# Strassen sums of the second feed-forward matrix made by adding DMAs instead of VectorE subtractions, with the signs turned and another order of products

## The chip, the cores and the metric

One Trainium2 chip, one of its NeuronCores. The metric is the device time of one execution in microseconds (us), median of several runs; lower is better. The engines are named as in the profile: PE (TensorE matmul, PEld its weight loads), ACT (ScalarE), DVE (VectorE), POOL (GpSimd), SP (SyncE, which issues most DMAs).

## The reference, cut to what matters

```python
x = x + mix @ w_out                                  # attention mix, before this
h2 = rmsnorm(x, norm2_w)
x = x + jnp.square(jax.nn.relu(h2 @ w_ff1)) @ w_ff2  # the feed-forward pair
return rmsnorm(x, final_norm_w)
```

x is 512 x 1024 in fp32, w_ff1 1024 x 4096, w_ff2 4096 x 1024. All products are to fp32 accuracy.

## The kernel before, in words

A product to fp32 accuracy is made of three fast ones. Each weight tile of 128 x 1024 is loaded as fp32 (wraw or w2raw) and cut in two (`parts`): ACT copies it, rounded, into wh, and DVE writes wl = raw - wh. The activations are cut alike (Ah and Al, yh and yl). PE then adds up wh by Ah, wh by Al and wl by Ah in PSUM. One such pair (wh, wl) is called a piece here.

The feed-forward part goes in four chunks (NC = 4, here 0 to 3). A chunk has eight tiles of the first matrix (`ff1`, tiles f of 0 to 31; PE writes bank f, ACT makes relu and square into h), and then one multiplication of a 512 x 1024 activation block by a 1024 x 1024 block of w_ff2 (`ff2`). Since that block is cut in 2 x 2 quadrants on each side, seven products do the work of eight (Strassen, in Winograd's form). The products are numbered 0 to 6. Each takes sums or differences of the activation quadrants (`a_parts`: s1 to s4, from h) and of the weight quadrants (`sums2`: b11, b12, b21, b22, each of two tiles ip = 0, 1). Piece "6.1" below is tile ip = 1 of the weights of product 6. Each product is 24 matmuls, 12 for each half q of its 256 rows. Its PSUM banks are called X, Y, Z and W; when a bank is whole enough, DVE adds it into x3 (`add`), the tile of the result. PE goes one tile of ff1 into the next chunk before each chunk's products, and in the last chunk straight from f = 31 to the products.

The order of all instructions on all engines is set by `Plan`, a small model of the engines that runs while the kernel is built: streams of work (loads, cuts, sums, products) each offer their next instruction, and the one that could start earliest by the model's costs is written next. The order is then fixed; on the chip every engine takes its instructions in that order and waits on semaphores. A stream also takes and gives counted buffers: `big` (23 tiles of 128 x 1024, for raw tiles, pieces and sums), `w` (5 pieces at a time, 10 in the last chunk), `raw2` (loaded w_ff2 tiles, 8) and the PSUM banks.

What the change touches. `fetch2` loads the four quadrants of a chunk with eight SP DMAs. `sums2` waits for them, and DVE makes the four sums as b12 - b11, b22 - that (a tile of its own, t2), t2 - b11 and b21 - t2, two tiles each: 8 subtractions of 128 x 1024 in a chunk. `products` gives the order in which `cut2` cuts the weights and `ff2` multiplies: 0, 1, 2, 3, 4, 5, 6 in chunks 0 to 2, and 0, 4, 1, 6, 2, 3, 5 in chunk 3. In chunk 3 the last additions into x3 feed the final norm: ACT squares and sums a tile (junk), DVE makes the mean (m), ACT and DVE the inverse root (y, tmp), and DVE and ACT the output (of, xw), which SP stores. POOL multiplies four finished halves of x3 by the norm weights (xw, `weighted`), and is otherwise idle in the feed-forward part.

Of the kernel before, what the change touches and what calls it, by code (L numbers as in the profile page):

```python
# [32 lines left out]
class Op:  # L33


    def __init__(self, eng, method, args, kw):
        self.eng, self.method, self.args, self.kw = eng, method, args, kw
        self.out = args[0]
        outs = [args[0]]
        inner = [a for a in list(args[1:]) + [v for k, v in kw.items() if k != "accum_out"] if isinstance(a, bass.AP)]  # L40
        if kw.get("accum_out") is not None:
            outs.append(kw["accum_out"])
        if method == "tensor_tensor_reduce":
            outs.append(inner.pop())
        self.outs = [o.tensor.name for o in outs]
        self.ins = [a.tensor.name for a in inner]
# [24 lines left out]
        if method == "dma_start":  # L71
            self.cost = 0.06
            self.size = 4 * n * args[0].shape[0]


# [114 lines left out]
def hybrid_block_kernel(ctx: ExitStack, tc: tile.TileContext, xT_d, x_d, w0_d, wv_d, wqk_d, wo_d, w1_d, w2_d,  # L190
# [9 lines left out]
    plan = Plan(nc, dict(BANKS, raw=3, w=WPAIRS, big=BIGS, raw2=8, part=5, lev=4, cnt=1))  # L200
    spawn, fire, give = plan.spawn, plan.fire, plan.give
    late = dict(copy=LC, tt=LT)

# [104 lines left out]

    quads = {}

    def fetch2():
        yield ("wait", ("raw", ("1", 5)))
        for c in range(NC):
            for q in ((0, 0), (1, 0), (1, 1), (0, 1)):
                for ip in range(2):
                    yield ("take", "raw2")
                    yield ("take", "big")
                    t = quads[c, q, ip] = big("w2raw")
                    yield SP.dma_start(t, w2_d[c, q[0], q[1], ip])
                fire(("quad", c, q))  # L320
            spawn(sums2(c), 4)

    def sums2(c):

        for q in ((0, 0), (1, 0), (1, 1), (0, 1)):
            yield ("wait", ("quad", c, q))
        b11, b12, b21, b22 = ([quads.pop((c, q, ip)) for ip in range(2)] for q in ((0, 0), (0, 1), (1, 0), (1, 1)))
        t2 = [None, None]
        B[c] = {0: b11, 1: b21, 5: b22, 3: b12, 2: t2, 4: b11, 6: b21}
        for n in (0, 1, 5):  # L330
            fire(("B", c, n))
        if c == NC - 1:
            yield ("prio", 2)
        for ip in range(2):
            yield DVE.tensor_tensor(b12[ip], b12[ip], b11[ip], op=OP.subtract)
            yield ("take", "big")
            t2[ip] = big("t2")
            yield DVE.tensor_tensor(t2[ip], b22[ip], b12[ip], op=OP.subtract)
        fire(("B", c, 2))
        fire(("B", c, 3))  # L340
        yield ("wait", ("cut2", c, 0))
        for ip in range(2):
            yield DVE.tensor_tensor(b11[ip], t2[ip], b11[ip], op=OP.subtract)
        fire(("B", c, 4))
        yield ("wait", ("cut2", c, 1))
        for ip in range(2):
            yield DVE.tensor_tensor(b21[ip], b21[ip], t2[ip], op=OP.subtract)
        fire(("B", c, 6))
        yield ("wait", ("cut2", c, 2))
        give("big")  # L350
        give("big")

    B = {}

    def products(c):


        if c < NC - 1:
            return ((0, "X", True, ((0, 0),)), (1, "Y", True, ((0, 0),)), (2, "X", False, ((0, 1),)), (3, "Z", True, ((1, 1),)),
                    (4, "X", False, ((1, 1),)), (5, "Z", False, ((0, 1),)), (6, "X", False, ((1, 0),)))  # L360
        return ((0, "X", True, ((0, 0),)), (4, "W", True, ((1, 1),)), (1, "Y", True, ((0, 0),)), (6, "W", False, ((1, 0),)),
                (2, "X", False, ((0, 1), (1, 1), (1, 0))), (3, "Z", True, ((1, 1),)), (5, "Z", False, ((0, 1),)))

    def cut2(c):
        for o, (n, *_) in enumerate(products(c)):
# [7 lines left out]
                yield from parts(("2", c, n, ip), B[c][n][ip])  # L373
            fire(("cut2", c, n))
            for _ in range(2):
                if n > 2:
                    give("big")
                    give("raw2")

# [612 lines left out]
    def a_parts(c, h):  # L992
# [28 lines left out]
        for f in range(4):
            yield ("wait", ("h", c, f))
        for ip in range(2):
            yield from split(0, ip, quad(0, one, ip))
        for ip in range(2):
# [3 lines left out]
        yield from urgent(1)  # L1029
        if c == NC - 1:  # L1030
            for ip in range(2):
                yield from split(4, ip, s3[ip])
        yield from urgent(2)
        for f in range(4, 8):
            yield ("wait", ("h", c, f))
        for ip in range(2):
            yield from split(1, ip, quad(1, one, ip))
        if c == NC - 1:
            yield from urgent(3)
            for ip in range(2):  # L1040
                yield from split(6, ip, quad(1, two, ip))
        yield from urgent(4)
        for ip in range(2):
            s1[ip], s2[ip] = new("s1"), new("s2")
            for i in range(2):
                yield DVE.tensor_tensor(s1[ip][:, i], quad(0, two, ip)[i], quad(1, two, ip)[i], op=OP.add)
                yield DVE.tensor_tensor(s2[ip][:, i], s1[ip][:, i], quad(0, one, ip)[i], op=OP.subtract)
        for ip in range(2):
            yield from split(2, ip, s2[ip])
        yield from urgent(5)  # L1050
        for ip in range(2):
            yield from split(3, ip, s1[ip])
        yield from urgent(6)
        for ip in range(2):
            s4[ip] = new("s4")
            for i in range(2):
                yield DVE.tensor_tensor(s4[ip][:, i], quad(1, one, ip)[i], s2[ip][:, i], op=OP.subtract)
        if c < NC - 1:
            for ip in range(2):
                yield from split(4, ip, s3[ip])  # L1060
        for ip in range(2):
            yield from split(5, ip, s4[ip])
        if c < NC - 1:
            for ip in range(2):
                yield from split(6, ip, quad(1, two, ip))

    A = {}
    TAGS = dict(X="s", Y="pt", Z="pt", W="mm")

    def add(c, i, q, acc):  # L1070
        n, b_, _, targets = products(c)[i]
        for blk, half in targets:
            t = 2 * blk + q
            if c == NC - 1 and n != 5:
                yield ("prio", 1.3 + i + 2 * (n == 4))
            yield DVE.tensor_tensor(x3[t, half], acc, x3[t, half], op=OP.add)
# [39 lines left out]
    def ffn():  # L1116
# [219 lines left out]
```

## Time and profile before

| | |
|---|---|
| runs | 595.39, 594.39, 595.22 us, median 595.22 us |
| profiled execution: its span, first to last instruction | 592.2 us |
| median less span: what lies around the span | 3.0 us |
| PE clock granted, mean | 0.996 |
| bytes moved by DMA | 61.91 MB |

The profiled execution's own time is known as its span; the 3.0 us are what the median of the runs has beyond it. In the rows below, a row of a timeline or of the chain of waits starts with its start in the span and its duration, both in us; in a table of windows each engine has its busy time and its count of instructions, and at the end stand the granted clock, the busy share of the DMA engines and their GB/s. A row of the costliest groups or of one tile says how many instructions there are of a form and how long they take.

### The profile page before, as it was taken

The numbers are of one execution on the slowest core, as the hardware profiler recorded it, in microseconds if no ns is written. First come the engines' busy times: TensorE is split into PE (matmuls) and PEld (weight loads), VectorE is DVE, ScalarE is ACT, GpSimd is POOL, SyncE is SP. The second block draws the span as 40 slices with busy tenths as digits, with TensorE's granted clock in tenths as the row PEclk, the third lists the DMA queues.
The fourth block names the chain that finished last, engine by engine and source line by source line (L and its number), as shares of the span: only waits on it lengthen the run. The fifth ranks groups of instructions, "written<-read, shape, count | busy, mean of one in ns | idle before, by whom it ended". The sixth has DMA issues, their size and how long they took to land.

```text
span 592.2 us, 8140 instructions
## 1 busy us (share of the span) xinstructions
PE 579.9 (98%) x3021; PEld 477.9 (81%) x3021; DVE 424.9 (72%) x829; ACT 324.7 (55%) x603; POOL 17.6 (3%) x33
## 2 busy tenths in 40 slices
PE   9999999999999999999999999999999999999993
PEld 8978888778877777899888888888888888888882
DVE  5879995854897824566579954499925799665995
ACT  6744256865687734555456424565244564365534
POOL 6020000000000000000000000000000000000020
PEclk9999999999999999999999999999999999999998
DMA  8921404132314610093104732015521046200003
GB/s 294 346 75 37 141 21 143 53 107 71 109 57 125 246 35 2 11 384 139 37 0 143 243 113 71 1 71 199 191 72 35 2 143 212 72 0 37 1 0 143
DMA packets 20391, 61.91 MB, mean 105 GB/s; under 512 B 2544, under 2 KB 2586, under 8 KB 20352
## 3 DMA queue, kind: packets, MB, share of 16 engines
q1 hardware_dynamic: 19728, 60.37, 29.7%
q0 software_dynamic: 480, 1.02, 0.5%
q8 instruction: 24, 0.39, 0.3%
q14 instruction: 15, 0.12, 0.1%
q10 hardware_dynamic: 144, 0.01, 0.0%
HBM read 59.25 MB, written 2.13 MB: 104 GB/s over the span
## 4 chain that ended last, share of the span: by engine, by line
PE 86%; DVE 10%; ACT 2%; issue 1%
PE f L123 30%; PE f2X L123 11%; PE qkps L123 8%; PE ops L123 7%; PE vps L123 7%; PE f2Z L123 6%; PE f2Y L123 3%; PE po L123 2%; PE ptp L123 2%; PE sps L123 2%; PE av L123 2%; DVE wl L123 2%; DVE x L123 2%; PE lp L123 1%; DVE P L123 1%; DVE Al L123 1%
## 5 line engine op out<-in xcount | busy, mean ns | idle before, releaser
L123 PE MATMUL f<-yh,wh 128*128 128x512 f32 (+1 forms) x288 | 105.3, 366 | 0.0
L123 PE MATMUL f<-yl,wh 128*128 128x512 f32 (+1 forms) x288 | 105.3, 365 | 0.0
L123 PE MATMUL f<-yh,wl 128*128 128x512 f32 (+1 forms) x288 | 105.2, 365 | 0.0
L123 DVE TENSOR_TENSOR wl<-wraw,wh 128x1024 fp32r<-128x1024 f32 (+1 forms) x68 | 78.4, 1161 | 33.5 <-ACT wh L123 28.0
L123 ACT ACTIVATE wh<-wraw 128x1024 fp32r<-128x1024 f32 (+1 forms) x67 | 67.2, 1013 | 60.1 <-PE f L123 24.0
L123 DVE TENSOR_TENSOR wl<-w2raw,wh 128x1024 fp32r<-128x1024 f32 x48 | 59.4, 1243 | 48.2 <-ACT wh L123 44.4
L123 ACT ACTIVATE wh<-w2raw 128x1024 fp32r<-128x1024 f32 x48 | 50.3, 1054 | 48.2 <-PE f L123 38.8
L123 PEld LDWEIGHTS f<-yh,wh 128*128 128x128 f32 x288 | 54.3, 189 | 8.8
L123 PEld LDWEIGHTS f<-yh,wl 128*128 128x128 f32 x288 | 54.3, 189 | 8.7
L123 PEld LDWEIGHTS f<-yl,wh 128*128 128x128 f32 x288 | 54.3, 189 | 8.7
L123 PE MATMUL f2X<-wh,Ah 128*128 128x512 f32 x112 | 43.6, 389 | 0.0
L123 PE MATMUL f2X<-wh,Al 128*128 128x512 f32 x112 | 43.6, 389 | 0.0
L123 PE MATMUL f2X<-wl,Ah 128*128 128x512 f32 x112 | 43.6, 389 | 0.0
L123 PE MATMUL qkps<-xh,wh 128*128 128x512 f32 x96 | 39.8, 415 | 0.0
L123 PE MATMUL qkps<-xh,wl 128*128 128x512 f32 x96 | 37.6, 391 | 0.0
L123 PE MATMUL qkps<-xl,wh 128*128 128x512 f32 x96 | 37.5, 391 | 0.0
L123 ACT ACTIVATE P<-P,mn 128x512 f32<-128x512 f32 (+3 forms) x48 | 26.6, 555 | 9.9 <-DVE mn L123 9.6
L123 DVE CUSTOM_DVE_ANT_0 P<-sps,nb 128x512 f32<-128x512 f32 (+3 forms) x48 | 22.2, 482 | 10.9 <-PE sps L123 10.8
L123 ACT ACTIVATE Ah<-s 128x512 fp32r<-128x512 f32 x32 | 19.6, 621 | 18.5 <-DVE s L123 18.5
L123 ACT ACTIVATE h<-f 128x512 f32<-128x512 f32 x32 | 18.6, 582 | 18.3 <-PE f L123 18.3
L123 PE MATMUL vps<-wh,xh 128*128 128x512 f32 x64 | 27.2, 424 | 0.0
L123 PE MATMUL ops<-wh,mh 128*128 128x512 f32 x64 | 26.1, 407 | 0.0
(223 smaller groups left out, 1191.6 us busy)
## 6 DMA issues: line engine op xcount, KB each, us to landing
wraw<-in_w SPq DMA_DIRECT2D x32, 512.0 KB, 3.3
w2raw<-in_w SPq DMA_DIRECT2D x32, 512.0 KB, 4.0
wraw<-in_wqk SPq DMA_DIRECT2D x12, 512.0 KB, 4.1
wraw<-in_wv SPq DMA_DIRECT2D x8, 512.0 KB, 5.4
wraw<-in_wo SPq DMA_DIRECT2D x8, 512.0 KB, 3.5
nb<-tab SPq DMA_DIRECT2D x12, 256.0 KB, 3.5
wraw<-in_w SPq DMA_DIRECT2D x8, 264.0 KB, 7.0
xT<-in_xT SPq DMA_DIRECT2D x8, 256.0 KB, 7.0
```

Of the source, the lines that this page charges most:

```text
L123: getattr(getattr(self.nc, op.eng), op.method)(*op.args, **op.kw)
```

## The change: what it does

- The weight sums are made by DMAs that POOL issues with `accum_op=add`: such a DMA reads a quadrant from DRAM and adds it to what stands in the tile in SBUF. Quadrant b12 is loaded twice (tiles of products 3 and 4), so a chunk has 10 loads instead of 8, and 8 adding DMAs of 512 KB in chunks 0 to 2 and 12 in chunk 3. The 32 subtractions on DVE, and the tile t2, are gone. `raw2` grows to 10.
- The sums become plain sums: 3 is b12 + b11, 4 is b12 + b22, 2 is b12 + b11 + b22, 6 is 2's sum + b21. In chunks 0 to 2 one tile holds 3, then 2, then 6: each DMA adds in place after the earlier product's piece has been cut from the tile. In chunk 3, 6 is made in the tile of 4 by two more additions (b11, b21), and 3 in the tile of b11.
- The signs move to the activations (s1 is a difference, s4 a sum) and to `add`, which subtracts the bank from x3 for some products.
- Chunks 0 to 2 take the products in the order 0, 3, 2, 1, 4, 5, 6; chunk 3 keeps its order. `a_parts` makes what each product needs in that order. Bank Y moves from the tag pt to o and g.
- `Plan` counts an adding DMA as 1.0 us of POOL, and as a reader of its tile.

```diff
+        self.ins = [a.tensor.name for a in inner] + (self.outs if "accum_op" in kw else [])
...
+            self.cost = 1.0 if "accum_op" in kw else 0.06
...
+    plan = Plan(nc, dict(BANKS, raw=3, w=WPAIRS, big=BIGS, raw2=10, part=5, lev=4, cnt=1))
...
     def sums2(c):
-        for ip in range(2):
-            yield DVE.tensor_tensor(b12[ip], b12[ip], b11[ip], op=OP.subtract)
-            yield ("take", "big")
-            t2[ip] = big("t2")
-            yield DVE.tensor_tensor(t2[ip], b22[ip], b12[ip], op=OP.subtract)
...
+        def plus(n, q):
+            for ip in range(2):
+                yield POOL.dma_start(B[c][n][ip], w2_d[c, q[0], q[1], ip], accum_op=OP.add)
+
+        b = B[c]
+        if c < NC - 1:
+            yield from plus(3, (0, 0))
+            yield from plus(4, (1, 1))
+            yield ("wait", ("cut2", c, 3))
+            b[2] = b[3]
+            yield from plus(2, (1, 1))
+            yield ("wait", ("cut2", c, 2))
+            b[6] = b[2]
+            yield from plus(6, (1, 0))
+        else:
+            yield from plus(4, (1, 1))
+            b[2] = b[3]
+            yield from plus(2, (0, 0))
+            yield ("wait", ("cut2", c, 4))
+            b[6] = b[4]
+            yield from plus(6, (0, 0))
+            yield from plus(2, (1, 1))
+            yield from plus(6, (1, 0))
+            yield ("wait", ("cut2", c, 0))
+            b[3] = b[0]
+            yield from plus(3, (0, 1))
...
-                if n > 2:
+                if n in ((0, 1, 4, 5, 6) if c < NC - 1 else (1, 2, 3, 5, 6)):
                     give("big")
                     give("raw2")
...
+            yield DVE.tensor_tensor(x3[t, half], x3[t, half], acc, op=OP.subtract if half and b_ in "XW" else OP.add)
```

Three places in the built order. First POOL in the last chunk, after the change. Tiles 4870 and 4879 (ip = 0 and 1) hold 4 and then 6, tiles 4819 and 4829 hold 2, tiles 4536 and 4545 hold b11 and then 3. Before the change POOL has nothing at this place, only the four xw multiplications behind it.

```order
L123 DMA w2raw_4870<-in_w2 128x1024
L123 DMA w2raw_4879<-in_w2 128x1024
L123 DMA w2raw_4819<-in_w2 128x1024
L123 DMA w2raw_4829<-in_w2 128x1024
L123 DMA w2raw_4870<-in_w2 128x1024
L123 DMA w2raw_4879<-in_w2 128x1024
L123 DMA w2raw_4819<-in_w2 128x1024
L123 DMA w2raw_4829<-in_w2 128x1024
L123 DMA w2raw_4870<-in_w2 128x1024
L123 DMA w2raw_4879<-in_w2 128x1024
L123 DMA w2raw_4536<-in_w2 128x1024
L123 DMA w2raw_4545<-in_w2 128x1024
```

So between the first addition for 6 (fifth and sixth row) and the second (ninth and tenth) stand the two that finish 2.

Second, ACT and DVE in the last chunk around the cut of 6. Before the change, on ACT: wh_5240 and wh_5259 are pieces 6.0 and 6.1, wh_5275 is 2.0, the h are ff1's results of f = 28 to 31, the Ah cuts for products 1 and 6.

```order
L123 ACTIVATE wh_5240<-w2raw_4807 128x1024
L123 ACTIVATE h_5242<-f1_5199 128x512
L123 ACTIVATE h_5242<-h_5242 128x512
L123 ACTIVATE Ah_5256<-h_5121 128x256
L123 ACTIVATE Ah_5256<-h_5169 128x256
L123 ACTIVATE wh_5259<-w2raw_4822 128x1024
L123 ACTIVATE Ah_5268<-h_5205 128x256
L123 ACTIVATE wh_5275<-t2_4936 128x1024
```

The same place on ACT after the change; 6.0 is wh_5255 and 6.1 wh_5279, from the tiles that POOL's DMAs add to.

```order
L123 ACTIVATE h_5248<-f1_5204 128x512
L123 ACTIVATE h_5248<-h_5248 128x512
L123 ACTIVATE Ah_5265<-h_5134 128x256
L123 ACTIVATE wh_5255<-w2raw_4870 128x1024
L123 ACTIVATE Ah_5265<-h_5175 128x256
L123 ACTIVATE wh_5279<-w2raw_4879 128x1024
L123 ACTIVATE Ah_5286<-h_5208 128x256
L123 ACTIVATE Ah_5286<-h_5248 128x256
```

6.0 has moved behind the last h, and both copies of 6 still stand ahead of the activations' cuts Ah_5286 for product 1.

On DVE before the change the low halves of 6.0 and 6.1 (wl_5241 and wl_5260) both stand ahead of the additions of product 0 (f2X) into x3:

```order
L123 TENSOR_TENSOR wl_5241<-w2raw_4807,wh_5240 128x1024
L123 TENSOR_TENSOR Al_5257<-h_5121,Ah_5256 128x256
L123 TENSOR_TENSOR Al_5257<-h_5169,Ah_5256 128x256
L123 TENSOR_TENSOR wl_5260<-w2raw_4822,wh_5259 128x1024
L123 TENSOR_TENSOR x3_2310<-f2X_5235,x3_2310 128x512
L123 TENSOR_TENSOR Al_5269<-h_5205,Ah_5268 128x256
```

After the change (wl_5256 and wl_5280):

```order
L123 TENSOR_TENSOR wl_5256<-w2raw_4870,wh_5255 128x1024
L123 TENSOR_TENSOR Al_5266<-h_5175,Ah_5265 128x256
L123 TENSOR_TENSOR x3_2310<-x3_2310,f2X_5241 128x512
L123 TENSOR_TENSOR Al_5287<-h_5208,Ah_5286 128x256
L123 TENSOR_TENSOR x3_2314<-x3_2314,f2X_5242 128x512
L123 TENSOR_TENSOR Al_5287<-h_5248,Ah_5286 128x256
L123 TENSOR_TENSOR Al_5306<-h_5134,Ah_5305 128x256
L123 TENSOR_TENSOR Al_5306<-h_5175,Ah_5305 128x256
L123 TENSOR_TENSOR Al_5315<-h_5208,Ah_5314 128x256
L123 TENSOR_TENSOR Al_5315<-h_5248,Ah_5314 128x256
L123 TENSOR_TENSOR wl_5280<-w2raw_4879,wh_5279 128x1024
```

The low half of 6.1 has moved behind the additions of product 0 and six cuts of activations.

Third, DVE where product 3 (f2Z) ends and product 5 waits for its bank. Before:

```order
L123 TENSOR_SCALAR m_5503<-ssq_5495 128x1
L123 TENSOR_TENSOR x3_2325<-f2X_5236,x3_2325 128x512
L123 TENSOR_SCALAR m_5518<-ssq_5514 128x1
L123 TENSOR_TENSOR x3_2322<-f2Z_5483,x3_2322 128x512
L123 TENSOR_TENSOR x3_2327<-f2Z_5484,x3_2327 128x512
```

After:

```order
L123 TENSOR_SCALAR m_5518<-ssq_5510 128x1
L123 TENSOR_TENSOR x3_2325<-x3_2325,f2X_5242 128x512
L123 TENSOR_TENSOR x3_2322<-x3_2322,f2Z_5491 128x512
L123 TENSOR_SCALAR m_5536<-ssq_5532 128x1
L123 TENSOR_TENSOR x3_2327<-x3_2327,f2Z_5492 128x512
```

The first addition of f2Z and the small m, which waits for ACT, have changed places.

More of the change, by code (lines that the diff above doesn't have):

```diff
@@ L45, in __init__ @@
         self.outs = [o.tensor.name for o in outs]
-        self.ins = [a.tensor.name for a in inner]
+        self.ins = [a.tensor.name for a in inner] + (self.outs if "accum_op" in kw else [])
         n = 1
@@ L71, in __init__ @@
         if method == "dma_start":
-            self.cost = 0.06
+            self.cost = 1.0 if "accum_op" in kw else 0.06
             self.size = 4 * n * args[0].shape[0]
@@ L199, in hybrid_block_kernel @@
     BANKS = dict(mm=2, s=2, pt=2, o=1, g=1)
-    plan = Plan(nc, dict(BANKS, raw=3, w=WPAIRS, big=BIGS, raw2=8, part=5, lev=4, cnt=1))
+    plan = Plan(nc, dict(BANKS, raw=3, w=WPAIRS, big=BIGS, raw2=10, part=5, lev=4, cnt=1))
     spawn, fire, give = plan.spawn, plan.fire, plan.give
@@ L309, in hybrid_block_kernel @@
     quads = {}
+    SUMS = {3: (0, 1), 4: (1, 1)}
     def fetch2():
@@ L313, in fetch2 @@
         for c in range(NC):
-            for q in ((0, 0), (1, 0), (1, 1), (0, 1)):
+            B[c] = {}
+            for n, q in ((0, (0, 0)), (1, (1, 0)), (3, (0, 1)), (4, (0, 1)), (5, (1, 1))):
+                t = []
                 for ip in range(2):
@@ L317, in fetch2 @@
                     yield ("take", "big")
-                    t = quads[c, q, ip] = big("w2raw")
-                    yield SP.dma_start(t, w2_d[c, q[0], q[1], ip])
-                fire(("quad", c, q))
+                    t.append(big("w2raw"))
+                    yield SP.dma_start(t[ip], w2_d[c, q[0], q[1], ip])
+                B[c][n] = t
+                if n not in SUMS:
+                    fire(("B", c, n))
+                else:
+                    fire(("B0", c, n))
             spawn(sums2(c), 4)
@@ L323, in sums2 @@
     def sums2(c):
[L325 to L333, printed above, removed]
-        for ip in range(2):
-            yield DVE.tensor_tensor(b12[ip], b12[ip], b11[ip], op=OP.subtract)
-            yield ("take", "big")
-            t2[ip] = big("t2")
-            yield DVE.tensor_tensor(t2[ip], b22[ip], b12[ip], op=OP.subtract)
@@ L339, in sums2 @@
[L339 to L351, printed above, removed]
+        def plus(n, q):
+            for ip in range(2):
+                yield POOL.dma_start(B[c][n][ip], w2_d[c, q[0], q[1], ip], accum_op=OP.add)
@@ new lines, in sums2 @@
+        b = B[c]
+        if c < NC - 1:
+            yield from plus(3, (0, 0))
+            fire(("B", c, 3))
+            yield from plus(4, (1, 1))
+            fire(("B", c, 4))
+            yield ("wait", ("cut2", c, 3))
+            b[2] = b[3]
+            yield from plus(2, (1, 1))
+            fire(("B", c, 2))
+            yield ("wait", ("cut2", c, 2))
+            b[6] = b[2]
+            yield from plus(6, (1, 0))
+            fire(("B", c, 6))
+        else:
+            yield from plus(4, (1, 1))
+            fire(("B", c, 4))
+            b[2] = b[3]
[4 more added lines that the diff above has]
+            yield from plus(2, (1, 1))
+            fire(("B", c, 2))
+            yield from plus(6, (1, 0))
+            fire(("B", c, 6))
+            yield ("wait", ("cut2", c, 0))
+            b[3] = b[0]
+            yield from plus(3, (0, 1))
+            fire(("B", c, 3))
@@ L358, in products @@
         if c < NC - 1:
-            return ((0, "X", True, ((0, 0),)), (1, "Y", True, ((0, 0),)), (2, "X", False, ((0, 1),)), (3, "Z", True, ((1, 1),)),
+            return ((0, "X", True, ((0, 0),)), (3, "Z", True, ((1, 1),)), (2, "X", False, ((0, 1),)), (1, "Y", True, ((0, 0),)),
                     (4, "X", False, ((1, 1),)), (5, "Z", False, ((0, 1),)), (6, "X", False, ((1, 0),)))
@@ L1019, in urgent, with sum1, sum2, sum3 @@
                 yield ("prio", 1.4 + o)
[L1021 to L1025, printed above, removed]
+        def sum1(ip):
+            s1[ip] = new("s1")
+            for i in range(2):
+                yield DVE.tensor_tensor(s1[ip][:, i], quad(0, two, ip)[i], quad(1, two, ip)[i], op=OP.subtract)
+        def sum2(ip):
+            s2[ip] = new("s2")
+            for i in range(2):
+                yield DVE.tensor_tensor(s2[ip][:, i], s1[ip][:, i], quad(0, one, ip)[i], op=OP.subtract)
+        def sum3(ip):
             s3[ip] = new("s3")
@@ L1028, in a_parts @@
                 yield DVE.tensor_tensor(s3[ip][:, i], quad(0, one, ip)[i], quad(0, two, ip)[i], op=OP.subtract)
[L1029 to L1052, printed above, removed]
@@ L1053, in a_parts, with sum4 @@
-        yield from urgent(6)
-        for ip in range(2):
+        def sum4(ip):
             s4[ip] = new("s4")
             for i in range(2):
-                yield DVE.tensor_tensor(s4[ip][:, i], quad(1, one, ip)[i], s2[ip][:, i], op=OP.subtract)
-        if c < NC - 1:
+                yield DVE.tensor_tensor(s4[ip][:, i], quad(1, one, ip)[i], s2[ip][:, i], op=OP.add)
+        made = {0: (None, lambda ip: quad(0, one, ip)), 1: (None, lambda ip: quad(1, one, ip)), 2: (sum2, s2.get),
+                3: (sum1, s1.get), 4: (sum3, s3.get), 5: (sum4, s4.get), 6: (None, lambda ip: quad(1, two, ip))}
@@ L1059, in a_parts @@
+        for f in range(4):
+            yield ("wait", ("h", c, f))
+        for o, (n, *_) in enumerate(products(c)):
+            if o:
+                yield from urgent(o)
+            if o == (1 if c < NC - 1 else 2):
+                for f in range(4, 8):
+                    yield ("wait", ("h", c, f))
+            if n == 2 and not s1:
+                for ip in range(2):
+                    yield from sum1(ip)
             for ip in range(2):
-                yield from split(4, ip, s3[ip])
@@ L1061, in a_parts @@
-        for ip in range(2):
-            yield from split(5, ip, s4[ip])
-        if c < NC - 1:
+                if made[n][0] and not (n == 3 and s1.get(ip)):
+                    yield from made[n][0](ip)
             for ip in range(2):
-                yield from split(6, ip, quad(1, two, ip))
+                yield from split(n, ip, made[n][1](ip))
     A = {}
-    TAGS = dict(X="s", Y="pt", Z="pt", W="mm")
+    TAGS = dict(X="ss", Y="og", Z=("pt", "pt"), W=("mm", "mm"))
     def add(c, i, q, acc):
@@ L1075, in add @@
                 yield ("prio", 1.3 + i + 2 * (n == 4))
-            yield DVE.tensor_tensor(x3[t, half], acc, x3[t, half], op=OP.add)
+            yield DVE.tensor_tensor(x3[t, half], x3[t, half], acc, op=OP.subtract if half and b_ in "XW" else OP.add)
             if c == NC - 1 and not any((blk, half) in p[3] for p in products(c)[i + 1:]):
@@ L1083, in add @@
         if not any(p[1] == b_ and not p[2] for p in products(c)[i + 1:]):
-            give(TAGS[b_])
+            give(TAGS[b_][q])
         fire(("add", c, b_, q))
@@ L1151, in ff2 @@
                     if new:
-                        yield ("take", TAGS[b_])
-                        bk[b_, q] = bank(TAGS[b_], "f2" + b_)
+                        yield ("take", TAGS[b_][q])
+                        bk[b_, q] = bank(TAGS[b_][q], "f2" + b_)
                     else:
```

## The prediction

> **What bounds the kernel now.** I read the page first for the shares, then a table of windows over the feed-forward part, then the chain of waits from there to the end. The page's first lines:
>
> ```profile
> span 592.2 us, 8140 instructions
> PE 579.9 (98%) x3021; PEld 477.9 (81%) x3021; DVE 424.9 (72%) x829; ACT 324.7 (55%) x603; POOL 17.6 (3%) x33
> ```
>
> PE is busy in 98% of the span, so DVE's 72% could be in nobody's way. A share over the whole span doesn't settle that; the windows do. The first is nearly all of the feed-forward part, the second the end, the third a stretch in which w_ff2 loads stream.
>
> ```profile
> 262.00:577.00 315.00, 315.00 (x1454) 263.58 (x1454) 230.47 (x326) 157.33 (x239) 4.52 (x4) 1.00 0.26 90
> 577.00:592.20 15.20, 6.10 (x26) 4.43 (x24) 7.68 (x25) 7.23 (x22) 1.05 (x1) 0.83 0.37 139
> 256.00:264.00 8.00, 8.00 (x70) 8.00 (x69) 5.19 (x14) 5.70 (x14) 0.00 (x0) 1.00 1.01 411
> ```
>
> In 315.00 us PE works 315.00 us at the full granted clock. All weight sums of w_ff2 are made in this window, and none of them makes PE wait. What is left to gain or lose lies where PE stops, at 577. The chain of waits shows what PE does by stages, and then what leads to that stop:
>
> ```profile
> 460.90 7.71 PE f L123 x34
> 468.61 5.44 PE f2X L123 x24
> ...
> 479.49 5.44 PE f2X L123 x24
> ...
> 506.69 37.87 PE f L123 x167
> ```
>
> ```profile
> 549.61 0.65 DVE x L123
> ...
> 570.61 1.14 DVE wl L123
> ...
> 576.00 0.61 DVE x L123
> ...
> 577.39 0.04 DVE m L123
> ...
> 577.47 0.70 DVE x L123
> ```
>
> A product or a tile of ff1 is 24 matmuls in 5.44 us. From 549.61 on DVE is on the chain almost without a break, until the addition at 577.47 that frees bank Z for product 5. PE's timeline shows what hangs on it:
>
> ```profile
> 576.34 0.39 PE L123 MATMUL f2Z<-wl,Ah 128*128 128x512 f32 x1
> ...
> 578.31 0.47 PE L123 MATMUL f2Z<-wh,Ah 128*128 128x512 f32 x1 [0.90 <-DVE x L123]
> ```
>
> The first half's bank is whole at 576.34 + 0.39 = 576.73, but DVE adds it only at 577.47, since the m ahead of it waits for ACT. All that follows (norm, output, stores) hangs on this addition, so I let the end move as this addition moves.
>
> **The change part by part.** The removed subtractions, from the view of the tile w2raw, with the two cuts of the same tiles:
>
> ```profile
> L123 ACT ACTIVATE wh<-w2raw x48: 1042/1055/1066, 283.5 to 564.7; 128x1024 fp32r<-128x1024 f32 x48
> L123 DVE TENSOR_TENSOR wl<-w2raw,wh x48: 1212/1222/2255, 284.6 to 570.5; 128x1024 fp32r<-128x1024 f32 x48
> L123 DVE TENSOR_TENSOR w2raw<-w2raw x8: 1217/1218/1225, 266.7 to 504.1; 128x1024 f32<-128x1024 f32 x8
> L123 DVE TENSOR_TENSOR t<-w2raw x8: 1217/1221/1226, 273.5 to 507.6; 128x1024 f32<-128x1024 f32 x8
> L123 DVE TENSOR_TENSOR w2raw<-t,w2raw x8: 1218/1218/1220, 291.1 to 527.9; 128x1024 f32<-128x1024 f32 x8
> L123 DVE TENSOR_TENSOR w2raw<-w2raw,t x8: 1218/1220/1221, 302.0 to 541.5; 128x1024 f32<-128x1024 f32 x8
> ```
>
> 32 times 1.22 us is 39 us less for DVE. The last begins at 541.5, before the unbroken chain on DVE starts, and PE never waits before 577; so these 39 us are worth 0. PE's own work is unchanged: 28 products of 24 matmuls in either order, with other banks for Y, and the turned signs cost the same instructions. The reordered activation sums come in time: in chunk 2 ff1's last needed tile (f = 23) ends at 468.61 - 5.44 = 463.2, product 3 starts at 474.05, and what lies between is ACT's and DVE's work of 3 to 4 us.
>
> Added are 8 loads and 36 adding DMAs of 512 KB. Of adding DMAs the trace has no row. The nearest are these:
>
> ```profile
> w2raw<-in_w SPq DMA_DIRECT2D x32, 512.0 KB, 4.0
> cst<-in_cst POOLq DMA_DIRECT2D x1, 514.0 KB, 6.3
> tab<-vals POOLq DMA_DIRECT2D x2, 15.0 KB, 1.7
> ```
>
> The smallest DMA of POOL that is hardly any data lands in 1.7 us; that is my fixed part. Streaming at 411 GB/s, 512 KB (0.524 MB) take 1.28 us; that is the lower bound d of the moving part, as if the addition were free. For the upper one I take POOL's 514 KB in a full machine, 6.3 - 1.7 = 4.6 us. I choose twice the plain time, d = 2.55 us, because an addition has to read the tile as well as the source; that is nearer to the lower row, as the bytes are. [...]
>
> In chunks 0 to 2 the pressing sum is 2, made in 3's tile. In chunk 2 piece 3.1 can be cut when PE ends tile f = 23, at 463.2: 1.06 on ACT and 1.22 on DVE, so the DMA can go at 465.5. Product 2 starts at 479.49, and ahead of it must come the cut of 2.1 (2.3 us) and an addition into x3 behind it on DVE (0.7 us): the sum has 11.0 us, and needs 1.7 + 2.55 = 4.3. Cost 0; if a sum took twice the 6.3, 12.6 us, it would be 1.6 us in each of three chunks. The other waits on the queues don't press either: POOL has nothing behind its DMAs but xw at 561; on SP the loads of wraw that now stand behind w2raw loads wait for PE's product 6 (to 506.69), while tile f = 30 is wanted by PE at 506.69 + 5 x 5.44 = 533.89.
>
> In chunk 3 it is tight. 6 gets two additions after 4 is cut from the tile. The low half of 4.1 takes a buffer that tile f = 29 is read from until 533.8, so it ends at 535.0. Then POOL issues for 6.1 the first addition, two for 2, the second for 6.0, and, after the first has landed, the second for 6.1: five that stream through the same engines, 535.0 + 1.7 + 5 x 2.55 = 549.45, and the load of fw (another 1.28 us) now falls into the same stretch: 550.75. Who waits: ACT's copy of 6.1, and behind it on ACT the cut Ah of ff1's h for product 1. DVE's rows set the limit, here with ACT's:
>
> ```profile
> 547.31 1.05 ACT L123 ACTIVATE wh<-w2raw 128x1024 fp32r<-128x1024 f32 x1
> 548.26 0.40 ACT L123 ACTIVATE Ah<-h 128x256 fp32r<-128x256 f32 x1
> ```
>
> ```profile
> 549.57 0.69 DVE L123 TENSOR_TENSOR x<-f2X,x 128x512 f32<-128x512 f32 x1
> 550.17 0.42 DVE L123 TENSOR_TENSOR Al<-h,Ah 128x256 fp32r<-128x256 f32 x1
> ```
>
> DVE can't add product 0 before 549.5, whatever it has gained; the Al behind it is due at 550.1, for which its Ah must start by 549.7 and the copy of 6.1 by 548.7 (0.95 from start to start). So 550.75 is 2.05 us late, and as DVE has no gap from there to 577, the end is 2.05 us later.
>
> DVE also has more to do in that stretch. Before, both low halves of 6 are done when it adds product 0; now 6.1's comes behind it, 1.14 us. The addition that ended at 576.61 ends at 577.7, and then the first f2Z addition comes at once, 0.2 us after 577.47 instead of 0.7 before it; the m, now behind it, holds the second, until ACT's 0.73 us on the tile before are over (577.7 + 0.75 = 578.5, against 577.47 + 0.6 = 578.1). Both squares go to ACT in turn, so the end moves by 0.4 us. The two-engine stretch that slows DVE stays as it is:
>
> ```profile
> 561.96 1.47 DVE L123 TENSOR_TENSOR Al<-s,Ah 128x512 fp32r<-128x512 f32 x1
> ...
> 563.42 2.25 DVE L123 TENSOR_TENSOR wl<-w2raw,wh 128x1024 fp32r<-128x1024 f32 x1
> ```
>
> ```profile
> 561.59 3.00 POOL L123 TENSOR_TENSOR xw<-x,fw 128x512 f32<-128x512 f32 x2 [523.72 <-DVE x L123]
> ```
>
> (2.25 instead of 1.22 beside POOL's xw, which have the same place in the new order.)
>
> Sum: 0 + 0 + 0.4 + 2.05 = 2.45 us on the profiled execution's span of 592.2, which makes 594.65. The median of the runs stands 3.0 us above the span, so the forecast is 595.22 + 2.45 = 597.7 us, slower by 0.41%.
>
> **The rivals.** A. The additions stream at nearly the plain rate. The limit is (548.7 - 535.0 - 1.7 - 1.28) / 5 = 2.14 us each; below it ACT waits for nothing and only the 0.4 us of order remain: 595.6 us, no measurable change. For it: the DMA engines are busy only a quarter of the time (0.26); against it: the tile must be read, and twice 1.28 is over the limit.
>
> B. DVE's work is not what ends last at 577, for instance because POOL's xw no longer meet the cuts (1.8 us less on DVE). Then, with sums in time, the first f2Z addition comes at 576.75, since m no longer precedes it: 0.7 us earlier, 594.5 us. That is also the most that can be gained, since PE's matmuls before it are unbroken: 0.12%, less than the 0.2% (1.2 us) that a measurement of this kernel can tell from no change.
>
> C. Additions are slow, 4.6 us each as the POOL row bounds them: 535.0 + 1.7 + 5 x 4.6 + 1.28 = 561.0, 12.3 us late, and 595.22 + 12.3 + 0.4 = 607.9 us. For it: nothing here shows how an addition pipelines; against it: that row shared a full machine, here the additions stand nearly alone.
>
> **How the numbers follow.** Forecast (late by some 1 to 5 us in the last chunk) 0.45, A 0.36, B 0.05, C 0.14. The forecast's lower end, d = 2.2, still reads as no change: 0.04 of it. So faster 0.04, same 0.41, slower 0.55. The range takes in B's end and the forecast with d up to 3.1 us (2.05 + 5 x 0.55 = 4.8, 600.5 us), and leaves out most of C: 594.6 to 600.8.
>
> **What would show it.** In the profile after: PE without a gap from 262 to 577 (right for the 0 of the 39 us); DVE near 386 us busy; adding DMAs in the table of issues landing 4 to 5 us after issue when alone, and later in 535 to 551. On ACT the copy of 6.1 starting near 551 after a wait for a DMA of w2raw, with DVE idle near 550; PE's product 5 starting near 580.7. Wrong if ACT's copy of 6.1 starts by 548.7 (A), if product 5 starts by 577.8 (B), or if PE stops before products 2 of chunks 0 to 2 or anywhere before 577.

## The result, and the profile after the change

| | before | after |
|---|---|---|
| runs, median | 595.07 us (594.39 to 595.39, 4 runs) | 600.19 us (599.38 to 602.02, 4 runs) |
| ratio | 1 | 1.0099, 95% interval 1.0086 to 1.0113 |
| span of the profiled execution | 592.2 us | 597.5 us |

The kernel became slower by 1.0%: 5.1 us between the medians, 5.9 us by the ratio, and 5.3 us between the two profiled executions (the one after is the fastest of its four runs, 599.38 us). The forecast was slower by 2.45 us. The direction and the place were as forecast; the size was not. First the page of the changed kernel:

```profile
span 597.5 us, 8221 instructions
PE 580.9 (97%) x3021; PEld 478.6 (80%) x3021; DVE 390.6 (65%) x797; ACT 325.6 (54%) x603; POOL 49.3 (8%) x69
```

DVE is 34.3 us less busy and the kernel is slower. The table of windows (columns as in the prediction) shows where: PE still has no gap from 262 to 577, and then works 1.46 us in the next 7.

```profile
262.00:577.00 315.00, 315.00 (x1452) 263.34 (x1451) 191.02 (x287) 157.01 (x234) 34.68 (x38) 1.00 0.62 162
577.00:584.00 7.00, 1.46 (x4) 1.16 (x4) 6.29 (x13) 2.61 (x8) 2.55 (x2) 0.88 0.01 2
```

The timeline of the changed kernel around the last chunk, in the order of the wait as it travels: POOL's issues of the additions, ACT's copies of 6.0 and 6.1, DVE's cut of an activation for product 1 behind the copy of 6.1, its low half of 6.1 and its first and last additions of bank Z, and PE's product 0 and product 5.

```profile
531.24 0.88 POOL L123 DMA_DIRECT2D w2raw<-in_w  x1 [33.48 <-DVE wl L123]
534.93 3.58 POOL L123 DMA_DIRECT2D w2raw<-in_w  x4 [2.81 <-DVE wl L123]
540.71 2.67 POOL L123 DMA_DIRECT2D w2raw<-in_w  x3 [2.21 <-DMA w2raw<-in_w]
...
548.23 1.06 ACT L123 ACTIVATE wh<-w2raw 128x1024 fp32r<-128x1024 f32 x1 [2.20 <-DMA w2raw<-in_w]
553.05 1.06 ACT L123 ACTIVATE wh<-w2raw 128x1024 fp32r<-128x1024 f32 x1 [3.45 <-DMA w2raw<-in_w]
...
554.44 0.42 DVE L123 TENSOR_TENSOR Al<-h,Ah 128x256 fp32r<-128x256 f32 x1 [2.96 <-ACT Ah L123]
557.06 1.22 DVE L123 TENSOR_TENSOR wl<-w2raw,wh 128x1024 fp32r<-128x1024 f32 x1
581.78 0.68 DVE L123 TENSOR_TENSOR x<-x,f2Z 128x512 f32<-128x512 f32 x1
589.78 0.69 DVE L123 TENSOR_TENSOR x<-x,f2Z 128x512 f32<-128x512 f32 x1 [0.22 <-PE f2Z L123]
...
544.26 0.39 PE L123 MATMUL f2X<-wh,Ah 128*128 128x512 f32 x1
582.60 0.77 PE L123 MATMUL f2Z<-wh,Ah 128*128 128x512 f32 x1 [5.54 <-DVE x L123]
583.17 0.63 PE L123 MATMUL f2Z<-wh,Al 128*128 128x512 f32 x1
583.60 0.63 PE L123 MATMUL f2Z<-wl,Ah 128*128 128x512 f32 x1
...
585.71 0.40 PE L123 MATMUL f2Z<-wh,Al 128*128 128x512 f32 x1
585.95 0.40 PE L123 MATMUL f2Z<-wl,Ah 128*128 128x512 f32 x1
```

The chain is the one forecast: ACT waits for 6.1's last addition until 553.05, not 550.75; DVE waits 2.96 us for the cut Ah that stands behind that copy on ACT; DVE adds bank Z at 581.78 instead of 577.47; PE stops for 5.54 us instead of 0.90. The last four lines hold something that the forecast did not have. After the stop the first matmuls of product 5 start 0.43 us apart (0.57 between the first two), and from 585.71 on they are 0.23 us apart again, as in the products ahead of the stop.

Between kernels I compare three steps, which take out that each execution reaches the last chunk at a slightly other time: from PE's first matmul of product 0 to DVE's first addition of Z, from there to DVE's last addition of Z, and from there to the end. In the profile of before these rows are:

```profile
544.61 0.39 PE L123 MATMUL f2X<-wh,Ah 128*128 128x512 f32 x1
577.47 1.29 DVE L123 TENSOR_TENSOR x<-f2Z,x 128x512 f32<-128x512 f32 x2
584.46 0.68 DVE L123 TENSOR_TENSOR x<-f2Z,x 128x512 f32<-128x512 f32 x1
```

So before the steps are 32.86, 6.99 and 7.74 us, and after 37.52, 8.00 and 7.72. That is +4.66, +1.01 and nothing, less the 0.35 us by which the second execution reached product 0 earlier: 5.3 us, the difference of the spans. Those 0.35 us arise ahead of the change: from PE's first matmul of the feed-forward part to product 0 it is 290.48 us before (254.13 to 544.61) and 290.49 after (253.77 to 544.26). 4.66 us have to be explained ahead of the first addition and 1.01 us behind it.

### The profile page after: what moved, and what is told of

Its sections match the earlier page's. It is cut to its first block, busy times and chain, and to the rows that moved or that the text cites. A ratio compares the mean times of both kernels' runs of the same rounds, so it can differ in the third digit from the quotient of the medians.

```text
span 597.5 us, 8221 instructions
## 1 busy us (share of the span) xinstructions
PE 580.9 (97%) x3021; PEld 478.6 (80%) x3021; DVE 390.6 (65%) x797; ACT 325.6 (54%) x603; POOL 49.3 (8%) x69
## 4 chain that ended last, share of the span: by engine, by line
PE 74%; DVE 11%; issue 7%; DMA 5%; ACT 2%; SPq 0%; POOL 0%; POOLq 0%; DVEq 0%; ACTq 0%
PE f L123 23%; PE f2X L123 8%; PE qkps L123 8%; PE ops L123 7%; PE vps L123 7%; PE f2Z L123 5%; DMA w2raw<-in_w 4%; DVE wl L123 2%; PE po L123 2%; PE ptp L123 2%; PE sps L123 2%; PE f2Y L123 2%; DVE x L123 2%; PE av L123 2%; DVE Al L123 2%
## 5 line engine op out<-in xcount | busy, mean ns | idle before, releaser
L123 DVE TENSOR_TENSOR wl<-w2raw,wh 128x1024 fp32r<-128x1024 f32 x56 | 69.5, 1241 | 59.8 <-ACT wh L123 42.7
L123 ACT ACTIVATE wh<-w2raw 128x1024 fp32r<-128x1024 f32 x56 | 58.9, 1056 | 45.4 <-PE f L123 25.8
L123 POOL DMA_DIRECT2D w2raw<-in_w x36 | 31.7, 990 | 474.2 <-DVE yl L123 226.4
L123 PE MATMUL f2Z<-wh,Ah 128*128 128x512 f32 x64 | 25.7, 402 | 5.5 <-DVE x L123 5.5
L123 DVE CUSTOM_DVE_ANT_0 P<-sps,nb 128x512 f32<-128x512 f32 (+3 forms) x48 | 22.3, 482 | 11.0 <-PE sps L123 10.9
```

The source lines that it names most:

```text
L123: getattr(getattr(self.nc, op.eng), op.method)(*op.args, **op.kw)
```

## The experiments

Theory: 6.1's last addition is late, and everything follows from it, the slow matmuls included. Rivals: the new order on DVE costs most; the adding DMAs cost through the load on the DMA engines, wherever they stand. All ratios are to the kernel before, in runs on the same chip.

**6's second additions ahead of 2's.** The same DMAs on the same queue, and the same order of instructions on the other engines.

```diff
-            yield from plus(2, (1, 1))
-            fire(("B", c, 2))
             yield from plus(6, (1, 0))
             fire(("B", c, 6))
+            yield from plus(2, (1, 1))
+            fire(("B", c, 2))
```

> The changed kernel, with 6's second additions (b21) issued ahead of 2's second (b22) in the last chunk; all else in the same order on every engine. Main theory: 6.1's first addition still lands at 540.5, the second is issued then and lands 5.3 us later, near 546, ACT's copy of 6.1 starts by 548.7, PE stops about 1 us before product 5 instead of 5.5, the matmuls behind it keep 0.23 us spacing, span 592.2 to 592.9, time 595.0 to 596.0 us (1.000 to 1.0015 of before). First rival (the new order on DVE, with the low half of 6.1 behind product 0's additions, costs most): copy of 6.1 early but PE still stops 4 us or more, time 598.5 us or more. Second rival (the stop comes from loaded DMA engines in general): as the first, since the same bytes move.

Measured: 594.30 us, ratio 1.0001 (0.9992 to 1.0010). Its timeline:

```profile
547.62 1.05 ACT L123 ACTIVATE wh<-w2raw 128x1024 fp32r<-128x1024 f32 x1
...
544.69 0.39 PE L123 MATMUL f2X<-wh,Ah 128*128 128x512 f32 x1
578.50 0.47 PE L123 MATMUL f2Z<-wh,Ah 128*128 128x512 f32 x1 [1.01 <-DVE x L123]
...
577.68 0.67 DVE L123 TENSOR_TENSOR x<-x,f2Z 128x512 f32<-128x512 f32 x1
584.98 0.68 DVE L123 TENSOR_TENSOR x<-x,f2Z 128x512 f32<-128x512 f32 x1
```

ACT's copy of 6.1 starts at 547.62 and carries no wait; PE stops 1.01 us. The steps are 32.99 and 7.30 us: +0.13 and +0.31 against before. So the new order on DVE costs 0.44 us, and the whole rest of the loss goes when 6.1 is in time. Both rivals fall: the order is unchanged here, and so are the bytes.

**The last chunk's sums on DVE.** Chunks 0 to 2 keep the adding DMAs.

```diff
-            yield from plus(4, (1, 1))
...
+            for ip in range(2):
+                yield DVE.tensor_tensor(b[4][ip], b[4][ip], b[5][ip], op=OP.add)
...
+                yield DVE.tensor_tensor(b[3][ip], b[3][ip], b[0][ip], op=OP.add)
...
+                yield DVE.tensor_tensor(b[2][ip], b[5][ip], b[3][ip], op=OP.add)
...
+                yield DVE.tensor_tensor(b[6][ip], b[1][ip], b[2][ip], op=OP.add)
```

> The changed kernel, with the sums of the last chunk made by DVE (8 plain sums of 128x1024, 2 in a tile of its own, 6 in the tile of 4); chunks 0 to 2 keep the adding DMAs, and from product 0's additions on DVE's order is the changed kernel's. Main theory: the whole loss is in the last chunk's late sums; ACT's copy of 6.1 comes by 548.7, PE stops about 1 us before product 5, time 595.0 to 596.0 us (1.000 to 1.0015 of before). Rivals: if the order on DVE or the adding DMAs of chunks 0 to 2 cost it, 598 us or more.

Measured: 594.49 us, ratio 1.0001 (0.9992 to 1.0010), PE's stop 1.01 us. The 24 adding DMAs of chunks 0 to 2 cost nothing that can be measured, as the 290.48 and 290.49 us above say too.

**Matmuls in the stop.** Twenty extra matmuls into a bank that nobody reads, on PE between products 3 and 5.

```diff
+                if end:
...
+                    for _ in range(20):
+                        mm = PE.matmul(dummy, A[c, n, 0][0][:, 0, :128], loaded["2", c, n, 0][0][:, :512], start=True, stop=True)
```

> The changed kernel, with 20 extra matmuls (128x512, into a bank that nobody reads, 4.5 us) on PE between product 3 and product 5, in the stop of 5.5 us. Main theory: in the changed kernel product 5 starts 4.3 us later than before but its first 7 matmuls come 0.43 us apart instead of 0.23, because PE stood still; with PE kept at work the 24 matmuls take 5.3 us from first to last start instead of 6.8, and the end comes 0.8 to 1.2 us earlier, about 599.2 us (ratio to before 1.007 to 1.008). Rival (the slow matmuls have another cause, or the last additions on DVE set the end anyway): no change, about 600.2 us, or a little over if the extra matmuls reach past the stop.

Measured: 599.27 us, ratio 1.0080 (1.0067 to 1.0093). By the runs alone that is not told apart from the changed kernel (1.0099, 1.0086 to 1.0113). The trace tells it apart:

```profile
582.83 0.50 PE L123 MATMUL f2Z<-wh,Ah 128*128 128x512 f32 x1 [0.96 <-DVE x L123]
...
582.11 0.67 DVE L123 TENSOR_TENSOR x<-x,f2Z 128x512 f32<-128x512 f32 x1
589.40 0.68 DVE L123 TENSOR_TENSOR x<-x,f2Z 128x512 f32<-128x512 f32 x1
```

Product 5's 24 matmuls take 5.37 us from first to last start, 6.76 in the changed kernel. From the first to the last addition of Z it is 7.29 us instead of 8.00. The slow matmuls behind the stop of 5.54 us cost 0.71 us of the 1.01; the other 0.30 is the m between the two additions, which the kernel with 6 first has too. That PE is 1.39 us faster here and only 0.71 of it reach the last addition is because that addition now has DVE's steps of the norm ahead of it and no longer waits for PE.

**The additions for 3 later, twice.** First I let the stream wait for the cut of 6 instead of the cut of 0:

```diff
-            yield ("wait", ("cut2", c, 0))
+            yield ("wait", ("cut2", c, 6))
```

> The changed kernel, with the two additions for product 3 in the last chunk waiting for the cut of 6 instead of the cut of 0, so that they are not on the queue behind 6.1's second addition. Main theory (6.1's second addition lands at 553 instead of 548.7, that delays DVE, and with it product 5): 6.1's landing came 4.9 us after 6.0's, where one addition (2.57 us) and the load of fw (1.28 us) explain 3.8; if the additions for 3 share the DMA engines with it, ACT's copy of 6.1 starts near 552.0 and the end is 0.8 to 1.1 us earlier than in the changed kernel, about 599.1 us. Rival (the queue is strictly first in, first out, and the 1.1 us are the load of fw or the fixed part): copy of 6.1 still at 553.0, time still about 600.2 us.

Measured: 599.66 us, ratio 1.0089 (1.0075 to 1.0102). This edit did not reach the chip: the wait stands in the planner's model, and the order on POOL, ACT and DVE is that of the changed kernel. The trace shows POOL issuing the same three DMAs in one go, 12 us before the copy of 6.1:

```profile
540.66 2.67 POOL L123 DMA_DIRECT2D w2raw<-in_w  x3 [1.94 <-DMA w2raw<-in_w]
```

So it is a repeat of the changed kernel and tells nothing of its question. The second attempt puts a real wait in front: POOL copies a column of the high half of 6.1 first.

```diff
+            hold = small("hold", (128, 1))
+            yield POOL.tensor_copy(hold, f32(loaded["2", c, 6, 1][0])[:, :1])
             yield from plus(3, (0, 1))
```

> The changed kernel, with the two additions for product 3 in the last chunk truly held back on POOL: a one-column copy of the high half of 6.1 stands ahead of them, so they issue near 554.5 instead of 541.8. In the changed kernel 6.1's last addition lands 4.9 us after 6.0's, where one addition (2.57 us) and the load of fw (1.28 us) explain 3.8. If the additions for 3 take part of the DMA engines' time from it, ACT's copy of 6.1 starts near 552.0 and the time is some 0.9 us under the changed kernel's (ratio to before 1.008 to 1.0085). If the queue works them off in turn, the copy stays at 553.0 to 553.4 and the ratio at 1.0090 to 1.0100. 3's own tiles land by 563, in time for their copies near 565.

Measured: 599.68 us, ratio 1.0098 (1.0085 to 1.0111).

```profile
554.32 0.18 POOL L123 COPY hold<-wh 128x1 f32<-128x1 f32 x1 [13.11 <-ACT wh L123]
554.56 1.78 POOL L123 DMA_DIRECT2D w2raw<-in_w  x2
...
553.20 1.06 ACT L123 ACTIVATE wh<-w2raw 128x1024 fp32r<-128x1024 f32 x1 [2.92 <-DMA w2raw<-in_w]
```

The additions for 3 now issue at 554.56, and the copy of 6.1 still starts at 553.20, against 553.05 in the changed kernel. What stood behind 6.1 on the queue took nothing from it. In the changed kernel the copy of 6.1 comes 4.8 us after that of 6.0, about 1 us more than one addition and the load of fw at the forecast's prices (3.8); the theory that the additions for 3 take this 1 us falls.

**fw behind the additions.** Its load is issued by POOL after all additions instead of by SP at 542.5.

```diff
-        yield ("wait", ("cut2", NC - 1, 1))
+        yield ("wait", ("B", NC - 1, 3))
...
-        yield SP.dma_start(fw, ...)
+        yield POOL.dma_start(fw, ...)
```

> The changed kernel, with the load of fw issued by POOL behind all additions instead of by SP at 542.5. If fw takes its 1.28 us of the DMA engines' time ahead of 6.1, as the forecast had it, the copy of 6.1 starts near 551.8 and the time is some 1.2 us under the changed kernel's (ratio to before 1.0070 to 1.0080); if it takes more than its share because it stands on another queue, near 551 and 1.0065. If it takes nothing from it, the copy stays near 553.1 and the ratio at 1.0090 to 1.0100. fw lands by 560, ahead of its first use at 566.

Measured: 598.54 us (597.16 to 600.11), ratio 1.0077 (1.0062 to 1.0092).

```profile
532.01 0.88 POOL L123 DMA_DIRECT2D w2raw<-in_w  x1 [33.38 <-DVE wl L123]
547.99 0.55 POOL L123 DMA_DIRECT2D fw<-in_fw  x1 [4.24 <-PE f2X L123]
...
551.83 1.06 ACT L123 ACTIVATE wh<-w2raw 128x1024 fp32r<-128x1024 f32 x1 [1.96 <-DMA w2raw<-in_w]
...
581.39 0.47 PE L123 MATMUL f2Z<-wh,Ah 128*128 128x512 f32 x1 [3.56 <-ACT junk L123]
```

By the runs alone it is hardly told apart from the changed kernel; the trace again says more. From POOL's first addition for 6 to the copy of 6.1 it is 551.83 - 532.01 = 19.82 us, in the changed kernel 553.05 - 531.24 = 21.81, and in the kernel with 3 behind 21.91. So fw's load cost 2.0 us there, not the 1.28 us that the forecast gave it. Most of that is the time of its own packets: by the table of queues they took 1.4 us of all 16 DMA engines in the kernel before (17.3% of the 8 us from 538) and 1.8 us beside the additions (6.0% of the 30 us from 530). Where the rest comes from these runs do not settle.

**Plain copies in the last chunk.** The 12 adding DMAs without `accum_op`, on the same queue. The additions are left out.

> The changed kernel, with the 12 adding DMAs of the last chunk as plain copies of the same bytes on the same queue in the same order: the additions are left out, and products 2, 3, 4 and 6 of that chunk use the quadrant loaded last. If an adding DMA takes twice a plain one's time on the DMA engines (2.57 against 1.3 to 1.5 us), the stretch of busy DMA engines from 537 to 556 shrinks to about 11 us, 6.1's second transfer lands by 546, ACT waits for nothing, and the ratio to before is 1.000 to 1.0015. If it is POOL's queue that moves 205 GB/s whatever the DMA does, the copy of 6.1 starts near 553 again and the ratio is 1.009 to 1.010.

Measured: 594.37 us, ratio 1.0004 (0.9995 to 1.0013). The windows of the two kernels, this one first (the last two columns are the busy share of the DMA engines and GB/s):

```profile
537.00:545.00 8.00, 8.00 (x37) 6.63 (x36) 2.45 (x2) 2.50 (x4) 1.81 (x4) 1.00 0.98 381
```

```profile
537.00:556.00 19.00, 19.00 (x85) 15.76 (x84) 6.59 (x10) 8.04 (x16) 4.17 (x5) 1.00 1.05 213
```

The DMA engines are fully busy in both (0.98 and 1.05), at 381 GB/s with plain copies and 213 with additions (fw's plain load among them). The table of queues for 530 to 560 has the same eight transfers on POOL's queue (packets, MB, share of the 16 engines' 30 us), first as plain copies, then as additions:

```profile
q0 software_dynamic: 1152, 4.19, 36.9%
```

```profile
q0 software_dynamic: 1152, 4.19, 74.3%
```

That is 11.1 and 22.3 us, 1.4 and 2.8 us each. An addition cost twice the DMA engines' time; it was not POOL's queue that was slow.

**A version meant to beat both.** On top of 6 first, the low half of 6.1 is put ahead of product 0's additions on DVE, and the m behind the second addition of Z.

```diff
+            if c == NC - 1 and n == 0:
+                yield ("wait", ("w", ("2", c, 6, 1)))
...
+            if hold:
+                yield ("wait", hold)
```

> 6's second additions ahead of 2's, as in the kernel with 6 first, and on DVE the low half of 6.1 ahead of product 0's additions and the last m of product 2 behind the second addition of product 3. If DVE's unbroken work from 549.5 to 577 is all that keeps PE's stop at 577 in place, taking 1.14 us out of it lets the first addition of bank Z come at 576.75 to 577.0 instead of 577.68, the m saves another 0.3 us behind it, and the time is 0.8 to 1.1 us under the kernel with 6 first, 0.1 to 0.2% under before (ratio 0.998 to 0.9995). If something else is late next, no change (1.000).

Measured: 596.43 us (595.09 to 599.13), ratio 1.0046 (1.0028 to 1.0064): slower, where a gain was expected. The edit also moved ACT's copy of 2.0 ahead of the cuts of h for product 1, and 2's second addition is now the late one:

```profile
553.39 1.06 ACT L123 ACTIVATE wh<-w2raw 128x1024 fp32r<-128x1024 f32 x1 [3.50 <-DMA w2raw<-in_w]
...
580.88 0.47 PE L123 MATMUL f2Z<-wh,Ah 128*128 128x512 f32 x1 [2.47 <-DVE x L123]
```

It is the same loss by another tile: whichever of 6 and 2 gets its additions last delays the copy that the order puts in front of product 1's cuts. (The profiled execution, 597.75 us, is one of the longer of the six, and about 1 us of it has nothing to do with the edit: its feed-forward part starts at 255.03, 0.90 us later than before, and its product 0 at 545.61, 1.00 us later.) To cure it, the next kernel issues both additions for 2 before the cut of 4, some 30 us earlier:

```diff
             yield from plus(2, (0, 0))
+            yield from plus(2, (1, 1))
+            fire(("B", c, 2))
             yield ("wait", ("cut2", c, 4))
             b[6] = b[4]
             yield from plus(6, (0, 0))
```

> The last kernel (low half of 6.1 ahead of product 0's additions, m behind), with both additions for 2 issued before the cut of 4, so that on the queue behind that cut stand 6's four additions first and no copy on ACT waits. There ACT's copy of 2.0 waited 3.5 us for 2's second addition, ahead of the cuts of h for product 1; here 2's sums are whole some 30 us earlier. If the late sum is all that cost that kernel its 4 us, DVE's additions of bank Z come at 576.75 to 577.0, PE stops less than 0.4 us at 577, and the ratio to before is 0.998 to 0.9995. If DVE is late by something else (its own work from 544 to 577), the addition stays near 577.7 and the ratio at 1.000.

Measured: 595.25 us, ratio 1.0016 (1.0007 to 1.0025).

```profile
516.88 1.06 ACT L123 ACTIVATE wh<-wraw 128x1024 fp32r<-128x1024 f32 x1 [2.40 <-DMA wraw<-in_w]
...
545.82 0.39 PE L123 MATMUL f2X<-wh,Ah 128*128 128x512 f32 x1
...
556.22 0.69 DVE L123 TENSOR_TENSOR x<-x,f2W 128x512 f32<-128x512 f32 x1 [0.74 <-PE f2W L123]
578.80 1.27 DVE L123 TENSOR_TENSOR x<-x,f2Z 128x512 f32<-128x512 f32 x2
```

No copy of 6 or 2 waits any more, and the m, now behind, gives back its 0.3 us (6.97 us from the first to the last addition of Z, 7.30 with 6 first). Yet the time is not lower, for two reasons that the rows show. From product 0 to the first addition of Z it is 578.80 - 545.82 = 32.98 us, as with 6 first (32.99): the 1.14 us taken out of DVE's work ahead of 556 turn into a wait for PE's product 4 (0.74 us; the addition of f2W comes 10.40 us after the start of product 0 in both kernels), and from 556 on DVE has no gap, so it is its work from there that sets the first addition of Z. And the additions of 2 now stand among the loads of wraw: ACT's copy of an ff1 tile waits 2.40 us for its load and starts at 516.88, where in the changed kernel it starts at 515.22 without a wait for a DMA. By the view of waits PE stops for the h that stands behind this copy on ACT, and product 0 comes 291.8 us after the start of the feed-forward part instead of 290.5:

```profile
PE f L123 <- ACT h L123: 1.0, 1, 1.0
```

No version here beats the kernel before; of those that make all the sums, 6 first and the last chunk on DVE equal it.

## Why the prediction was right or wrong, point by point

- *39 us of subtractions are worth 0.* Right: PE has no gap from 262 to 577. DVE is 390.6 us busy (forecast near 386): the 32 instructions are gone, but a row on DVE overlaps its neighbours a little in the trace (a low half of 1.22 us is followed after 1.14), so its busy time falls by 34.3 us, 1.07 us for each, and not by 39.
- *Chunks 0 to 2 cost 0.* Right: 1.0001 with the sums of the last chunk alone taken back to DVE, and product 0 of chunk 3 starts 290.48 us after the start of the feed-forward part before and 290.49 after.
- *The order on DVE costs 0.4 us (0.2 to the first addition of Z, then the m).* Right: 0.13 + 0.31 = 0.44 us in the kernel with 6 first.
- *The limit for the copy of 6.1, 548.7.* Right: with the copy at 547.62 nothing waits. In the changed kernel's own time it is 548.35, since product 0 starts 0.35 us earlier, and 553.05 is 4.70 us late; the first addition of Z is 4.66 us late, 0.13 of it by the order. So 4.53 us are the copy's, and the limit is right to 0.2 us.
- *6.1 ready at 550.75, 2.05 us late.* **This is the term that was mis-sized**: it measured 4.53 us at the first addition of Z. The moving part, 2.55 us for each addition, was right. POOL's issues and their landings, from the table of issues cut down to one issue at a time, are:

```profile
w2raw<-in_w POOLq DMA_DIRECT2D x1, 512.0 KB, 5.2
...
w2raw<-in_w POOLq DMA_DIRECT2D x1, 512.0 KB, 5.5
```

 The first row is 6.0's first addition (issued at 531.24, with nothing beside it), the second 6.1's (534.93): landed at 540.4, where the forecast had 535.0 + 1.7 + 2.55 = 539.25. The copy of 6.0, three additions later, starts at 548.23, so three took at most 7.8 us, 2.6 each against the 2.55 chosen. Twice the plain time is near what these runs show: 381 against 213 GB/s, a factor of 1.8, more without fw's plain bytes, and 2.0 in the engines' time (2.8 against 1.4 us). That the read of the tile makes the difference was the author's argument; no run shows the cause. What was too small are the two other terms. The fixed part is 5.2 - 2.6 = 2.6 us, not the 1.7 that a DMA of 15 KB showed: +1.2 us at the first landing. And fw's load costs 2.0 us, not 1.28: +0.7 us. With 0.1 for the additions' rate and 0.3 unexplained that is the 2.30 us from 550.75 to 553.05, and the earlier product 0 makes the other 0.35 us.
- *All that follows moves by as much as the addition of Z.* **Wrong by 0.71 us**: the longer stop itself made PE slower behind it (matmuls 0.43 us apart behind 5.54 us, 0.23 with the stop filled). No term of the forecast had this. Together: 4.53 + 0.44 + 0.71 - 0.35 = 5.3 us of span, against a forecast of 2.45.
- *The range, 594.6 to 600.8.* That 600.19 lies in it is luck as far as the cause goes: its upper part stood for additions of up to 3.1 us each, and they took 2.6. What filled it were the fixed part, fw's load and the slower matmuls, none of which had a spread there.
- *Rivals.* A (the additions stream at the plain rate, no loss) did not happen, but the kernel with plain copies shows that its condition was rightly put: 1.0004. B did not happen: POOL's xw still meets the low half (2.25 us at 568.15), and with the sums in time the first addition of Z came at 577.68 and not earlier. C was too dear: an addition takes 2.6 us, not 4.6.
- *What would show it.* The copy of 6.1 waiting for a DMA: yes, at 553 instead of near 551. Product 5 starting near 580.7: at 582.60. "Additions landing 4 to 5 us alone": 5.2.

## What to carry to other kernels

Moving sums from a busy engine to adding DMAs gains nothing where that engine only fills gaps beside PE (here DVE's 34.3 us less were worth 0), and puts the sum's latency (here 5.2 us alone, 2.6 us for each one queued ahead) wherever a piece is wanted soon after it can be made. Order such a queue by when each sum is wanted: swapping two pairs of lines brought back all that could be measured of the 1.0%. And when pricing a DMA, take the fixed part from one of the same size (fw's plain load of 512 KB, on SP's queue, landed in 3.8 us in the kernel before, which less the 1.4 us of its packets leaves 2.4, nearer to 2.6 than the 1.7), and count the loads of other queues that fall into the same stretch at more than their own time (fw's cost 2.0 us here, its packets took 1.8).

## What the runs showed of the hardware that was not expected

- **Behind some of PE's stops the granted clock was half, for 3.41 us in the changed kernel.** In the changed kernel 7 matmuls behind the stop of 5.54 us start 0.43 us apart (granted clock 0.50 from 582.5 to 585.5); with the stop filled (0.96 us left) they start 0.23 us apart (granted clock 1.00 from 583 to 586). In the trace of the changed kernel the clock falls at 582.28, rises at 585.69 (3.41 us later) and falls again at 592.52; in the 3.40 us from 578.80 to 582.20 PE worked 0.00 us. The length of the stop alone does not tell the cases apart: behind 2.47 us, in the kernel with both edits, the clock halved, and behind 3.56 us, in the kernel with fw behind, it did not. First the kernel with both edits, then the one with fw behind (PE's busy time is the number behind the length of the stretch, the granted clock the third from the end):

```profile
577.85:581.20 3.35, 0.88 (x5) 0.45 (x4) 3.35 (x7) 1.75 (x5) 2.19 (x2) 1.00 0.00 0
581.25:584.60 3.35, 3.35 (x10) 2.61 (x9) 2.51 (x12) 2.78 (x10) 0.31 (x1) 0.50 0.03 10
```

```profile
576.20:579.57 3.37, 1.63 (x8) 1.01 (x6) 3.37 (x6) 0.72 (x2) 0.64 (x1) 1.00 0.00 0
579.60:583.00 3.40, 1.61 (x7) 1.38 (x8) 2.49 (x8) 2.10 (x7) 1.89 (x2) 1.00 0.02 5
583.02:586.40 3.38, 3.38 (x16) 2.79 (x16) 2.88 (x10) 2.21 (x7) 0.00 (x0) 1.00 0.24 87
```

 In the first PE worked 0.88 us in the 3.35 us that the stop of 2.47 us lies in, and the next 3.35 us have a granted clock of 0.50. In the second the stop of 3.56 us falls on the first two windows, with 1.63 and 1.61 us of PE's work, and the clock is 1.00 in them and in the one behind. In the first attempt with 3 later, behind a stop of 5.57 us, the granted clock was 0.50 from 583 to 586. What decides whether the clock halves these traces do not show; no run moved a stop on purpose to test it.
- **An adding DMA took twice the DMA engines' time of a plain one**, 2.8 against 1.4 us for 512 KB (213 against 381 GB/s with all engines busy), and POOL needed 0.88 us to issue one of 512 KB (0.55 for a plain one, fw's). The loads beside them got slower too; medians from issue to landing in the changed kernel, which before were 4.0 us for w2raw, 3.3 for wraw and 3.8 for fw:

```profile
w2raw<-in_w SPq DMA_DIRECT2D x40, 512.0 KB, 5.6
w2raw<-in_w POOLq DMA_DIRECT2D x36, 512.0 KB, 7.7
wraw<-in_w SPq DMA_DIRECT2D x32, 512.0 KB, 5.9
...
fw<-in_fw SPq DMA_DIRECT2D x1, 512.0 KB, 10.6
```
